# Where the blocks of w_down are staged in layer 1's feed-forward network

## The chip, the cores and the metric

The kernel runs on one core of one Trainium2 chip. The metric is the device time of one execution in microseconds (us), the median over several runs. The engines are TensorE (PE, with its weight loads shown apart as PEld), VectorE (DVE), ScalarE (ACT), GpSimd (POOL) and SyncE (SP, which here only issues DMAs).

## What is computed

Two layers of a diffusion transformer on 512 image tokens and 256 context tokens, model width 1024, in float32. Each layer is an attention and Fourier mixer followed by a feed-forward network (FFN) of width 2816. In layer 1, the last one, the context isn't updated, so that its FFN works on the 512 image tokens alone:

```python
def swiglu(h, w_gate, w_up, w_down):
    return (jax.nn.silu(h @ w_gate) * (h @ w_up)) @ w_down
...
x = x + gt2 * swiglu(rms_norm(x, g_ffn[l]) * (1 + sc2) + sh2, w_gate[l], w_up[l], w_down[l])
...
return rms_norm(x, g_final)
```

## The kernel before

Every float32 product is made of three products of float32r parts: each operand is split into a high part (ACT casts it, `split`, L103) and a low part (DVE subtracts, also L103), and `mm3` (L90) multiplies high by high, high by low and low by high.

`ffn` (L1638 on; it runs for layer 1 only, layer 0 has a function of its own) cuts the width 2816 into eleven blocks of 256. Of block p it needs 256 columns of w_gate, 256 columns of w_up and 256 rows of w_down, 1 MB each; they are called G(p), U(p) and D(p) here. The program's order for p = 1 to 10 is:

1. G(p) through `seven`: a Strassen product with seven products of 12 matmuls (256 columns moving), 84 in all, then Silu (L1680, L1682).
2. D(p-1) is loaded and split (`load_down`, `load_cols`), and `down(p-1)` multiplies it with `us`, the split activations of block p-1: eight products (d = 0 to 7) of 6 matmuls with 512 columns moving, each added to the residual tile `xt[d]` by DVE (L1663).
3. U(p) through `seven`, its results multiplied with the gate's, and split into the `us` of block p (L1695 and L103).

Block 0 is made by `first`, without `seven`; the last block's `down` is done in two halves with the final norm behind them. The order that the engines really follow is set by a scheduler when the program is built: it takes instructions by the program's order, but lets a later one go ahead on an engine when an earlier one isn't ready yet by its own model of time. The queues are then fixed. SP issues the loads in that fixed order too, and an issue waits until the tile that it writes is free.

Tiles around the change:

- `raw` (L116): [128, 2048] float32 (1 MB), a ring of two, `tag="raw", bufs=2`. In `ffn` every G, U and D block is loaded into it. `load_pair` takes one for G and U, and `load_cols` (L119) one for D. A `raw` is free again when its last part is split. For G and U that is late: `weights` (L1296) has POOL make sums of quarters in place in the `raw` (L1316 to L1318, L1324), and the seven parts are split one by one as the products come to them.
- `w` (L106): [128, 1024], a ring of ten. Each of the seven parts takes one tile; D takes four, from its split until the last product of its `down`.
- `s1` in `weights` is on tag `hf`, a ring of two. `utile` (tag `u`, a ring of eight) holds the activations.
- `xt[k]` (L1170, in `w_out`): eight residual tiles of [128, 768]. In layer 1 only columns 0 to 511 are loaded (L1173), changed or read. They lie in the pool `fp`, which takes the place of the attention's pool `at` when `w_out` begins; a tile of `fp` can be written when the tiles of `at` that lay at its address are done.

Of the kernel before, what the change touches and what calls it, by code (L numbers as in the profile page):

```python
# [9 lines left out]
F32 = mybir.dt.float32  # L10
# [7 lines left out]
P = 128  # L18
D = 1024
KB = D // P  # L20
SX = 512
SC = 256
T = SX + SC
# [23 lines left out]
class Builder:  # L47
# [68 lines left out]
    def raw(self):  # L116
        return self.wp.tile([P, 2048], F32, name=self.nm("raw"), tag="raw", bufs=2)

    def load_cols(self, src, nk, w, per, slots=None):  # L119

        hs = []
        krow = src.rearrange("(k p) w -> p k w", p=P)
        step = min(nk, (2048 // w) // per * per)
        for k0 in range(0, nk, step):
            kn = min(step, nk - k0)
            r = self.raw()
            rv = r[:, 0 : kn * w].rearrange("p (k w) -> p k w", w=w)
            self.queue(rv, krow[:, k0 : k0 + kn, :])
            for s in range(0, kn, per):
                h, l = (slots or self.whl)()  # L130
                n = min(per, kn - s)
                for j in range(n):
                    c = slice(j * w, (j + 1) * w)
                    self.split(h[:, c], l[:, c], r[:, (s + j) * w : (s + j + 1) * w])
                    hs.append((h[:, j * w : (j + 1) * w], l[:, j * w : (j + 1) * w]))
        return hs
# [1028 lines left out]
    def w_out(self, l, oh, ol):  # L1165

        nc = self.nc
        full = l < DEPTH - 1
        w = self.a["w_out"][l]
        xt = [self.fp.tile([P, T], F32, name=self.nm("xt"), tag=f"x{k}", bufs=1) for k in range(KB)]  # L1170
        e = T if full else SX
        for d in range(KB):
            nc.sync.dma_start(xt[d][:, 0:e], self.xsc[:, d, 0:e])  # L1173
        acc = self.fp.tile([P, T], F32, name=self.nm("acc"), tag="acc", bufs=1)
        hs = [self.utile(F32) for k in range(KB)]

        def one(d, wt, rng, s):
            r0, r1 = rng
            ps = self.mm()[:, 0 : r1 - r0]
            wh, wl = wt  # L1180
            self.mm3(ps, [(wh[:, k], wl[:, k], oh[k][:, r0:r1], ol[k][:, r0:r1]) for k in range(KB)])
            nc.vector.scalar_tensor_tensor(
                xt[d][:, r0:r1], ps, self.gt(l, 0, d, s), xt[d][:, r0:r1], op0=ALU.mult, op1=ALU.add
            )
            self.stat_add(acc, xt[d], rng, d)

        rngs = (XR,) if full else XH
        late = []
        for dp in range(KB // 2):
            rv = self.load_pair(w[:, dp * 256 : (dp + 1) * 256])  # L1190
            for j in range(2):
                d = 2 * dp + j
                wt = self.pair_half(rv, j)
                if d >= KB - LATE:
                    late.append((d, wt))
                    continue
                one(d, wt, XR, 0)
                if full:
                    one(d, wt, CR, 1)
        bcs = []  # L1200
        for rng, bank in zip(rngs, (self.fl, self.mm)):
            for d, wt in late:
                one(d, wt, rng, 0)
            bcs.append(self.stat_bc(acc, rng, bank()))
        hi, lo = self.act
        n = (T if full else SX) // 2
        last = []
        r0, r1 = rngs[0]
        for k in range(KB):
            shf = self.sh(l, 1, k, 0)  # L1210
            with self.tc.issue_after(last[-2]) if k > 1 else ExitStack():
                nc.vector.scalar_tensor_tensor(
                    hs[k][:, r0:r1], xt[k][:, r0:r1], self.sc(l, 1, k, 0), bcs[0], op0=ALU.mult, op1=ALU.mult
                )
            nc.scalar.activation(hi[k][:, 0:n], hs[k][:, 0:n], AF.Identity, bias=shf)
            last.append(
                nc.vector.scalar_tensor_tensor(
                    lo[k][:, 0:n], hs[k][:, 0:n], shf, hi[k][:, 0:n], op0=ALU.add, op1=ALU.subtract
                ).ins
            )  # L1220
        for k in range(KB):
            nc.scalar.activation(hs[k][:, r0:r1], hs[k][:, r0:r1], AF.Identity, bias=self.sh(l, 1, k, 0))
        if full:
            for d, wt in late:
                one(d, wt, CR, 1)
        for rng, bc in zip(rngs[1:], bcs[1:]):
            for k in range(KB):
                self.norm_raw(hs[k], xt[k], bc, rng, l, k, 0)
        if full:
            bc = self.stat_bc(acc, CR)  # L1230
            for k in range(KB):
                self.norm_raw(hs[k], xt[k], bc, CR, l, k, 1)
        return xt, hs
# [403 lines left out]
    def ffn(self, l, xt, hs):  # L1637
        nc = self.nc  # L1638
        full = l < DEPTH - 1
        wg, wu, wd = (self.a[n][l] for n in ("w_gate", "w_up", "w_down"))  # L1640
# [4 lines left out]
        cols = lambda p: slice(p * 256, (p + 1) * 256)  # L1645
# [23 lines left out]
                        nc.sync.dma_start(self.xsc[:, d, r0:r1], xt[d][:, r0:r1])  # L1669
            return done.ins  # L1670

        load_down = lambda p: self.load_cols(wd[cols(p), :], 2, D, 1)
        us = utiles()
        room = [[acc[:, j * n : (j + 1) * n]] * 2 for j in range(2)]
        parts = lambda j, cs, sl: self.split(us[j][0][:, cs], us[j][1][:, cs], sl)
# [2 lines left out]
        for p in range(1, npc):  # L1678
# [13 lines left out]
            if p < npc - 1:  # L1692
                for j in range(2):
                    e = slice(0 if j else n, 2 * n)
# [13 lines left out]
        p = npc - 1  # L1708
# [176 lines left out]
```

## Time and profile before

| | us |
|---|---|
| median of 3 runs | 1558.27 (1555.56 to 1558.91) |
| the profiled execution | 1555.41 |
| its span, first to last instruction | 1553.6 |
| layer 1's `w_out` and FFN, from 1139 us of the span to its end | 414.6 |
| of that, from block 1's U to the issue of block 10's D and a little behind | 1204 to 1503 |

The rows are read so: each names an engine, a line of the kernel, an operation and its tiles (what is written, an arrow, what is read), with its time. In square brackets stands the time that the engine stood idle before it, and what that idle time ended with. "PEclk" is the granted TensorE clock as a share of full speed. Matmuls overlap in the trace, so that a busy time of PE is not a measure of its load, but idle time of PE is idle.

### The profile page before, as it was taken

How to read it: one execution, taken by the hardware profiler on the slowest of the kernel's cores; microseconds unless marked ns; L12 is line 12 of the kernel's file. 1: busy time of each engine (PE TensorE's matmuls, PEld its weight loads, DVE VectorE, ACT ScalarE, POOL GpSimd, SP SyncE). 2: the span in 40 equal slices, each digit the busy share in tenths (PEclk: the TensorE clock that was granted, in tenths of full speed). 3: DMA queues.
4: the chain of work that ended last, by engine and by line, in shares of the span. 5: the costliest groups of instructions: out<-in, count | busy, mean ns of one | idle time of the engine just before them, and what ended most of it. 6: DMA issues, size and time to landing. Idle time of an engine off the chain costs nothing.

```text
span 1553.6 us, 25611 instructions
## 1 busy us (share of the span) xinstructions
PE 1485.4 (96%) x9769; PEld 1363.6 (88%) x9769; DVE 1133.1 (73%) x1907; ACT 763.9 (49%) x1542; POOL 556.7 (36%) x463
## 2 busy tenths in 40 slices
PE   6989989999999999999999998999999999999997
PEld 3789967688999999999899978987799898988987
DVE  3767577753978878876887866667749778777775
ACT  3556566642744444444435545666637344444344
POOL 0354345310256656452000025353401444344432
PEclk9999999999999999999999999999999999999999
DMA  9510085851133543446883541065441423223221
GB/s 339 197 48 29 1 263 159 290 190 29 54 130 130 163 138 123 161 137 227 307 301 110 167 128 35 28 201 189 141 134 52 136 82 109 83 82 126 92 82 55
DMA packets 124298, 211.59 MB, mean 136 GB/s; under 512 B 6456, under 2 KB 87120, under 8 KB 119056
## 3 DMA queue, kind: packets, MB, share of 16 engines
q1 hardware_dynamic: 116320, 203.92, 38.2%
q0 software_dynamic: 7856, 6.04, 2.0%
q8 instruction: 77, 1.26, 0.3%
q14 instruction: 45, 0.37, 0.1%
HBM read 180.96 MB, written 28.97 MB: 135 GB/s over the span
## 4 chain that ended last, share of the span: by engine, by line
PE 69%; DVE 10%; DMA 8%; ACT 4%; POOL 4%; issue 4%; SPq 1%; POOLq 0%; DVEq 0%; ACTq 0%
PE mm L90 15%; PE lg L90 14%; PE fl L90 13%; DVE w L103 5%; PE mm L1506 4%; PE mm L945 4%; PE lg L1506 4%; PE mm L937 2%; ACT w L103 2%; PE fl L278 2%; DMA raw<-in_w_up_dram 2%; PE lg L833 2%; PE lg L841 2%; DMA ra<-in_w_ada_dram 2%; PE fl L1506 1%
## 5 line engine op out<-in xcount | busy, mean ns | idle before, releaser
L103 DVE TENSOR_TENSOR w<-raw,w 128x512 fp32r<-128x512 f32 (+1 forms) x336 | 314.7, 949 | 113.5 <-ACT w L103 108.1
L103 ACT CAST w<-raw 128x512 fp32r<-128x512 f32 (+1 forms) x336 | 228.5, 701 | 316.4 <-POOL raw L1324 94.1
L90 PE MATMUL lg<-ahi,w 128*128 128x384 f32 (+1 forms) x640 | 151.2, 312 | 6.9 <-DVE w L103 3.1
L90 PE MATMUL fl<-ahi,w 128*128 128x384 f32 (+1 forms) x640 | 153.5, 308 | 0.9 <-ACT acc L1385 0.9
L852 POOL TENSOR_TENSOR p<-p,rc 128x768 f32<-128x768 f32 (+2 forms) x84 | 111.4, 1344 | 116.9 <-DVE rc L850 105.3
L90 PE MATMUL lg<-th,w 128*128 128x384 f32 (+1 forms) x640 | 150.4, 311 | 1.4 <-DVE u L1448 1.2
L90 PE MATMUL mm<-u,w 128*128 128x512 f32 (+1 forms) x576 | 137.9, 378 | 3.9 <-DVE u L103 2.2
L339 POOL TENSOR_TENSOR rs<-ms,mhalf 128x8 f32<-128x8 f32 (+3 forms) x22 | 28.6, 1304 | 288.7 <-DVE ms L335 288.7
L90 PEld LDWEIGHTS lg<-ahi,w 128*128 128x128 f32 x640 | 111.5, 191 | 11.2 <-ACT w L103 5.1
L90 PE MATMUL fl<-w,ahi 128*128 128x256 f32 x576 | 115.0, 293 | 5.9 <-DVE w L103 3.8
L90 PEld LDWEIGHTS mm<-u,w 128*128 128x128 f32 x576 | 98.0, 190 | 20.9 <-DVE u L103 3.5
L90 PEld LDWEIGHTS lg<-th,w 128*128 128x128 f32 x640 | 111.7, 191 | 3.3 <-DVE u L1448 1.5
L90 PEld LDWEIGHTS fl<-ahi,w 128*128 128x128 f32 x640 | 112.0, 190 | 2.5 <-ACT acc L1385 1.1
L90 PE MATMUL mm<-ahi,w 128*128 128x256 f32 (+1 forms) x448 | 107.1, 330 | 0.0
L1324 POOL TENSOR_TENSOR raw<-raw 128x512 f32<-128x512 f32 x40 | 62.3, 1559 | 110.8 <-DVE w L103 110.8
L90 PEld LDWEIGHTS fl<-w,ahi 128*128 128x128 f32 x576 | 93.5, 196 | 8.0 <-DVE w L103 4.3
L103 DVE TENSOR_TENSOR t<-mm,t 128x512 fp32r<-128x512 f32 x108 | 74.0, 687 | 34.7 <-ACT t L103 34.0
L90 PE MATMUL lg<-tl,w 128*128 128x384 f32 (+1 forms) x320 | 99.3, 310 | 0.0
L90 PE MATMUL lg<-alo,w 128*128 128x384 f32 (+1 forms) x320 | 99.2, 310 | 0.0
L1316 POOL TENSOR_TENSOR s<-raw 128x512 f32<-128x512 f32 x40 | 54.6, 1366 | 123.3 <-DMA raw<-in_w_up_dram 75.8
L90 PE MATMUL fl<-alo,w 128*128 128x384 f32 (+1 forms) x320 | 98.7, 308 | 0.0
L844 DVE TENSOR_REDUCE neg<-lg 128x1 f32<-128x768 f32 (+2 forms) x96 | 80.7, 851 | 19.9 <-PE lg L841 19.0
(367 smaller groups left out, 3980.7 us busy)
## 6 DMA issues: line engine op xcount, KB each, us to landing
raw<-in_w_ada_dram SPq DMA_DIRECT2D x40, 1024.0 KB, 4.9
raw<-in_w_gate_dram SPq DMA_DIRECT2D x22, 1024.0 KB, 5.2
raw<-in_w_up_dram SPq DMA_DIRECT2D x22, 1024.0 KB, 5.3
uh<-uh SPq DMA_DIRECT2D x33, 384.0 KB, 4.8
w<-uh SPq DMA_DIRECT2D x33, 384.0 KB, 4.6
wd<-in_w_down_dram SPq DMA_DIRECT2D x47, 256.0 KB, 5.1
raw<-in_w_in_dram SPq DMA_DIRECT2D x11, 1024.0 KB, 5.5
raw<-in_w_down_dram SPq DMA_DIRECT2D x11, 1024.0 KB, 4.8
```

The lines of the kernel that those rows point to most:

```text
L90: mm = lambda a, b, **k: self.nc.tensor.matmul(out, a, b, skip_group_check=more, **k)
L103: return self.nc.scalar.copy(hi, src).ins, self.nc.vector.tensor_sub(lo, src, hi).ins
L278: end = nc.tensor.matmul(st["ps"][o : o + 32, :], self.ct[:, k0 + i, :], rs[i][:, j], start=(k0 % hold == 0), stop=((k0 + by) % hold == 0) ...
L833: nc.tensor.matmul(o, qt[:, qs], K1[:, kv, k0 : k0 + w], start=True, stop=False)
L841: nc.tensor.matmul(o, qt[:, qs], K2[:, kv, k0 : k0 + w], start=False, stop=True)
L844: nc.vector.tensor_reduce(ng, lv, axis=AX.X, op=ALU.max, negate=True)
L852: nc.gpsimd.tensor_tensor(pt, pt, rc[:, i : i + 1].to_broadcast(list(pt.shape)), op=ALU.mult)
L937: nc.tensor.transpose(ps[:, col + j * P : col + (j + 1) * P], pt[:, c : c + P], self.ident)
L945: nc.tensor.matmul(out[:, r], V[:, kb, kv, :], t[:, c], start=first and n == 0, stop=end and n == len(todo) - 1,)
L1316: nc.gpsimd.tensor_add(s1, a21, a22)
L1324: nc.gpsimd.tensor_sub(a12, a12, a11)
L1506: nc.tensor.matmul(ps, w[:, x, c], u[:, y], start=(not more and k == 0 and j == 0), stop=(k == npc - 1 and j == 2), skip_group_check=True,)
```

## The change

D's blocks get a tile of their own, `rd`, [128, 2048], one buffer, on the pool `fp`; `load_cols` takes the function that makes the tile as an argument. G and U keep the ring of two between them. The eight residual tiles of layer 1 become 512 wide instead of 768, 1 KB less for each partition and tile, 8 KB in all, which is what `rd` takes (2048 float32).

```diff
-    def load_cols(self, src, nk, w, per, slots=None):
+    def load_cols(self, src, nk, w, per, slots=None, raw=None):
...
-            r = self.raw()
+            r = (raw or self.raw)()
...
-        xt = [self.fp.tile([P, T], F32, name=self.nm("xt"), tag=f"x{k}", bufs=1) for k in range(KB)]
         e = T if full else SX
+        xt = [self.fp.tile([P, e], F32, name=self.nm("xt"), tag=f"x{k}", bufs=1) for k in range(KB)]
...
-        load_down = lambda p: self.load_cols(wd[cols(p), :], 2, D, 1)
+        own = lambda: self.fp.tile([P, 2 * D], F32, name=self.nm("rd"), tag="rd", bufs=1)
+        load_down = lambda p: self.load_cols(wd[cols(p), :], 2, D, 1, raw=own)
```

## Rows read from the trace of the kernel before

**Rows 1.** The page: busy time of each engine, its share of the span, and its instructions.
```profile
PE 1485.4 (96%) x9769; PEld 1363.6 (88%) x9769; DVE 1133.1 (73%) x1907; ACT 763.9 (49%) x1542; POOL 556.7 (36%) x463
```
**Rows 2.** Busy time by stretch, from layer 1's w_out to the end, and four stretches of two blocks each, from one issue of a G to the next but one. Columns: the stretch, its length, then busy us (and instructions) of PE, PEld, DVE, ACT and POOL, the granted clock, the DMA engines' share, GB/s.
```profile
1139.00:1553.60 414.60, 394.75 (x2746) 366.14 (x2744) 314.27 (x502) 184.16 (x362) 146.25 (x114) 0.99 0.27 90
...
1206.72:1272.48 65.76, 62.90 (x416) 57.34 (x415) 48.40 (x73) 26.84 (x49) 25.62 (x20) 0.97 0.30 102
1272.48:1336.45 63.97, 63.12 (x434) 58.28 (x434) 51.24 (x75) 26.91 (x50) 27.32 (x20) 1.00 0.30 99
1336.45:1403.50 67.05, 64.62 (x434) 59.65 (x433) 51.01 (x75) 27.17 (x50) 27.12 (x20) 0.97 0.29 95
1403.50:1468.89 65.39, 63.44 (x434) 58.32 (x433) 51.70 (x75) 26.97 (x50) 27.78 (x20) 1.00 0.29 98
```
**Rows 3.** The order in time of SP's DMA issues, in the third of these stretches. The start of each, its length, the line, the tile and the source.
```profile
1333.01 0.37 SPq L142 DMA_DIRECT2D raw<-in_w_up_dram  x1
1336.45 0.37 SPq L142 DMA_DIRECT2D raw<-in_w_gate_dram  x1
1351.42 0.37 SPq L114 DMA_DIRECT2D raw<-in_w_down_dram  x1
1362.78 0.37 SPq L142 DMA_DIRECT2D raw<-in_w_up_dram  x1
1366.01 0.37 SPq L142 DMA_DIRECT2D raw<-in_w_gate_dram  x1
1382.42 0.37 SPq L114 DMA_DIRECT2D raw<-in_w_down_dram  x1
1400.06 0.37 SPq L142 DMA_DIRECT2D raw<-in_w_up_dram  x1
1403.50 0.37 SPq L142 DMA_DIRECT2D raw<-in_w_gate_dram  x1
```
**Rows 4.** DMA issues between 1204 and 1503 us: tile and source, KB of one, median us from issue to landing.
```profile
raw<-in_w_up_dram SPq DMA_DIRECT2D x10, 1024.0 KB, 5.0
raw<-in_w_down_dram SPq DMA_DIRECT2D x10, 1024.0 KB, 4.8
```
**Rows 5.** The order in time of what happens around the arrival of the U that was issued at 1362.78 us: the end of D's split before it, PE, POOL and ACT.
```profile
1364.77 1.22 DVE L103 TENSOR_TENSOR w<-raw,w 128x1024 fp32r<-128x1024 f32 x1
...
1367.18 1.42 PE L90 MATMUL mm<-u,w 128*128 128x512 f32 x5 [0.72 <-DVE u L103]
...
1368.94 1.28 POOL L1316 TENSOR_TENSOR s<-raw 128x512 f32<-128x512 f32 x1 [2.36 <-DMA raw<-in_w_up_dram]
1368.97 0.62 ACT L103 CAST w<-raw 128x512 fp32r<-128x512 f32 x1 [3.79 <-DMA raw<-in_w_up_dram]
...
1369.64 0.39 PE L90 MATMUL lg<-ahi,w 128*128 128x256 f32 x1 [1.03 <-ACT w L103]
```
**Rows 6.** Busy time by stretch at five arrivals of a U and behind two of them; columns as in rows 2.
```profile
1234.00:1239.00 5.00, 2.63 (x14) 1.57 (x12) 4.04 (x5) 1.48 (x3) 1.44 (x2) 1.00 0.73 228
1239.00:1242.00 3.00, 2.82 (x15) 2.26 (x16) 2.84 (x2) 1.17 (x4) 2.84 (x3) 0.87 0.92 317
1242.00:1245.00 3.00, 3.00 (x17) 3.00 (x17) 0.16 (x1) 1.37 (x3) 2.92 (x3) 0.56 0.01 3
...
1303.00:1306.00 3.00, 2.16 (x13) 1.46 (x11) 2.62 (x3) 1.69 (x4) 2.67 (x2) 1.00 0.95 322
...
1366.00:1371.00 5.00, 2.57 (x11) 1.49 (x11) 3.53 (x5) 1.68 (x4) 2.56 (x3) 0.99 0.89 301
1371.00:1374.00 3.00, 3.00 (x13) 2.81 (x14) 1.45 (x1) 0.39 (x1) 2.92 (x3) 0.50 0.01 2
...
1434.00:1438.00 4.00, 2.41 (x10) 1.42 (x10) 3.46 (x5) 1.68 (x4) 2.50 (x3) 1.00 1.04 336
...
1498.00:1503.00 5.00, 3.41 (x19) 2.33 (x18) 4.57 (x6) 1.69 (x4) 3.60 (x3) 1.00 0.95 327
```
**Rows 7.** PE alone by stretch, two stretches that lie between such arrivals: length, busy us, granted clock, the DMA engines' share, GB/s.
```profile
1272.50:1301.40 28.90, 28.90 (x201) 1.00 0.32 107
1336.50:1366.00 29.50, 29.50 (x207) 1.00 0.32 104
```
**Rows 8.** Who waited for whom between 1160 and 1553 us: the engine and line that waited, for what, us in total, times, the longest.
```profile
POOL s L1316 <- DMA raw<-in_w_up_dram: 47.4, 10, 9.2
...
ACT w L103 <- POOL raw L1324: 36.8, 18, 3.8
ACT w L103 <- DMA raw<-in_w_up_dram: 30.8, 10, 3.8
ACT w L103 <- PE lg L90: 23.5, 17, 2.9
```
**Rows 9.** The order in time at the next D, the one that was issued at 1382.42 us: the first cast and the last subtraction of its split.
```profile
1399.03 1.04 ACT L103 CAST w<-raw 128x1024 fp32r<-128x1024 f32 x1
...
1402.26 1.21 DVE L103 TENSOR_TENSOR w<-raw,w 128x1024 fp32r<-128x1024 f32 x1
```
**Rows 10.** The order in time where layer 1's residual tiles are loaded and first used.
```profile
1125.04 10.69 SPq L1173 DMA_DIRECT2D xt<-xsc  x8
...
1137.55 0.75 DVE L1182 SCALAR_TENSOR_TENSOR xt<-mm,ada,xt 128x512 f32<-128x512 f32 x1 [5.69 <-PE mm L90]
```
**Rows 11.** The order in time on PE where the last block's `down` begins.
```profile
1529.50 3.97 PE L90 MATMUL mm<-u,w 128*128 128x256 f32 x27 [0.48 <-ACT u L103]
```

## The prediction

> **What bounds the kernel now.** I read the page first: PE is busy for 96% of the span and DVE for 73% [rows 1]. PE is the bound, so that only PE's idle time and lost clock can be won. Next the busy time by stretch: layer 1's last part takes 414.6 us, of which PE is idle for 19.9, and four stretches of two blocks each take 65.76, 63.97, 67.05 and 65.39 us, with PE idle for 2.86, 0.85, 2.43 and 1.95 us and a granted clock of 0.97 in two of them [rows 2]. The reader is to see that the stretches differ though their work is the same.
>
> Third, SP's issues in time [rows 3]. The ring of two `raw` is handed on without a pause. The U at 1333.01 keeps its `raw` until D takes it at 1351.42 (18.4 us); the G at 1336.45 keeps its own until the next U at 1362.78 (26.3); that D until the next G at 1366.01 (14.6). Then 19.6, 34.1 and 21.1 us for the next three. These six stays add up to 134.1 us, and on two buffers that is 67.05 us, the whole stretch. So nothing is loaded ahead: each U is asked for only when G's last part, or in the other parity D's, has left a buffer.
>
> Fourth, what that costs PE. The U issued at 1362.78 lands some 5.0 us later [rows 4]. POOL, ACT and, behind the cast, PE wait for it: PE starts on U at 1369.64 after 1.03 us of idleness, and had already stood for 0.72 us at 1367.18, where only `down` was left to it and DVE was still splitting `us` [rows 5]. By stretch, the five places of this kind have PE idle for 2.37 + 0.18 (1234 to 1242), 0.84 (1303), 2.43 (1366), 1.59 (1434) and 1.59 us (1498): 9.0 in all. Behind two of them PE runs at a lower granted clock: 3 us at 0.56 and 3 us at 0.87 after 1239, 3 us at 0.50, the lower of the clock's two levels (1.2 GHz), after 1371, that is 1.32 + 0.39 + 1.50 = 3.2 us lost [rows 6]. Between such places PE has no idle time: 28.90 of 28.90 us and 29.50 of 29.50, at full clock [rows 7]. Over layer 1's FFN, POOL waited for a U ten times, 47.4 us in total, and ACT ten times, 30.8 us [rows 8]; those are engines that aren't the bound, and only the 9.0 us are PE's.
>
> **The change part by part.** *D leaves the ring.* The number of loads, splits, sums and matmuls stays what it is; only when loads may start changes. Without D's stays, 134.1 - 14.6 - 21.1 = 98.4 us are left on two buffers, 49.2 us for two blocks. That is below what PE needs for them, so the ring stops being the bound even if every stay is some 25% longer. In the trace, U could have been issued when the earlier U left, at 1351.42 in place of 1362.78, and so landed at about 1356.5, some 10 us before PE runs out of other work at 1366; the next G at 1362.78 in place of 1366.01.
>
> How much is that? What PE needs for two blocks I take from the stretch with the least idleness: 63.12 us busy, at clock 1.00 [rows 2]. Four stretches: 4 x 63.12 = 252.5 us against 262.17 (1206.72 to 1468.89), a gain of 9.7. The fifth place, at 1498, lies behind them and gives 1.6. Sum: 11.3 us. Adding up the places instead gives 9.0 + 3.2 = 12.2, the most there is. I take 11.3, since the first way leaves some small waits standing.
>
> *D in its single tile.* A D may be loaded only when the one before has been split. That split ends at 1364.77 + 1.22 = 1365.99 [rows 5], the next D would land by 1371 (4.8 us [rows 4]), and its own first cast comes only at 1399.03 [rows 9]. Some 28 us hide it, and its cost is nothing; with that cover gone it would be up to 4.8 us for each block. Behind D's issue in SP's queue stand the next U and G, whose buffers come free at 1382 and 1400 [rows 3], so an issue that waits until 1366 holds nobody up.
>
> The Trainium skill ("Trainium Kernel Development and Optimization", Best Practices) says to double-buffer, so that DMA overlaps compute; it speaks against a single tile, and by it the loads would be exposed. The rows just read don't bear it out here, since the other work between two D lies between load and use; it is rival 4.
>
> *The ring of w.* ACT already waits for PE to give up a tile there, 17 times, 23.5 us [rows 8]. D's four tiles of ten are held from its split to the end of its `down`. An earlier D can be split earlier and hold them longer. The trace shows no such case. From below: nothing, as G and U keep six of ten; from above: PE misses one part of each `seven` by the 0.84 us that it waited at 1303 [rows 6], 20 times, 16.8 us. I take zero, because in the stretches without waits [rows 7] four tiles are held by D as well, and PE still doesn't stand.
>
> *Narrower residual tiles.* No instruction changes, since only 512 columns were ever moved. What lies behind `xt` moves to other addresses, and so waits for other tiles of the attention. The first issue is at 1125.04, and DVE first uses `xt` at 1137.55 after it waited 5.69 us for PE, not for the load [rows 10]. The last of the eight issues comes by 1135.73; if the first had to wait that long it would land at 1140.8, 3.3 us late. Below, nothing is to be won, because nobody waited. I take zero and keep the 3.3 us for the range.
>
> *The tail.* The last `down` starts with 0.48 us of idleness while ACT splits the last `us` [rows 11]; none of that hangs on a load, so it moves forward as a whole.
>
> What is late next? PE itself, and behind it DVE: 51 us in 63 [rows 2].
>
> **The rivals.** 1. *The split of `us` takes the place of the load.* PE's 0.72 us at 1367.18 was a wait for DVE's split, not for U. If the fixed order puts `down` ahead of U at every block, ten waits of about 0.75 us stay: 7.5 of the 11.3, and the gain is 3.8: 1554.5 us. For it: the program names `down` before U. Against it: where U was there in time, no such wait is left [rows 7].
>
> 2. *The change doesn't do what it says.* If the scheduler puts the next D ahead of U in SP's queue, that issue waits for D's split, until 1366, and U is as late as before, or later: 1558 us. For it: program order. Against: the scheduler has let G and U go by their readiness already, as U stands right before the next G in the queue [rows 3].
>
> 3. *The ring of w, the slower side.* Place: the splits in `seven`. Price: the 16.8 us above, less the gain: 1558.3 + 5.5 = 1563.8. It decides from the point where one D is split while the four tiles of the D before are still held, so that G and U have two tiles for a product of 12 matmuls. For it: ACT's 23.5 us of waits for PE. Against: the splits of G and U come before the next D's in the program, and are ready more often once their loads are early.
>
> 4. *The single tile exposes D.* Ten times 4.8 us, less the gain: 1558.3 + 48 - 11.3 = 1595. It decides from the point where a D is split less than 5 us before the next is needed; the rows show 28 us [rows 9].
>
> **How the numbers follow.** The profiled execution took 1555.41 us, 2.9 less than the median of 1558.27 and near the fastest of the three. By its own time the forecast is 1555.4 - 11.3 = 1544.1; by the median, which is what is compared, 1558.3 - 11.3 = 1547.0. If the 2.9 us come from more clock lost at the same places, they go as well. Chances: the forecast 0.60, rival 1 0.15, rival 2 0.11, rival 3 0.11, rival 4 0.03. Faster by more than 0.2% (3.1 us, about what a measurement of this kernel can tell from no change) are the forecast and rival 1: 0.75; within it rival 2: 0.11; slower rivals 3 and 4: 0.14. The range: at its lower end all 12.2 us from the median and the 2.9 us largely too, against small new waits: 1542. At its upper end the forecast with 3.3 us for the residual tiles (1550.3), rival 1 and rival 2: 1558.5. Rivals 3 and 4 are left out.
>
> **What would show it.** In the changed kernel's trace: SP issues each U some 10 us or more before PE's first product of it; POOL's and ACT's waits for a U shrink from 47.4 and 30.8 us to a few; the stretches of two blocks come down to 63 to 64 us with the granted clock at 1.00; PE's idleness in the four of them falls from 8.1 to about 1 us, and the part before `w_out` is unchanged. Wrong would be: waits of PE for DVE's `us` at each block (rival 1), U's still issued right behind a D (rival 2), or more and longer waits of PE for the splits of `w` (rival 3).

## The result

The median fell from 1557.01 us (1555.56 to 1558.91, 4 runs) to 1548.52 us (1547.32 to 1550.48, 4 runs): a ratio of 0.9946 [0.9928, 0.9964], 8.5 us less by the medians. Forecast were 1547.0 us and a gain of 11.3. The profiled execution of the changed kernel took 1550.48 us, with a span of 1548.7. It is the slowest of its four, and everything ahead of layer 1's `w_out` ran later in it than in the profile of before, though the two kernels do the same there: the first load of `xt` is issued at 1127.54 us against 1125.04 [rows 10]. I therefore measure from that issue to the last addition into `xt`: 419.40 us before and 411.97 after, 7.43 less.

The busy times of the page hardly differ from [rows 1], as it should be: the same work is done, in less time.

```profile
PE 1485.8 (96%) x9769; PEld 1362.4 (88%) x9769; DVE 1121.1 (72%) x1907; ACT 763.5 (49%) x1542; POOL 553.6 (36%) x463
```

SP's issues of the changed kernel, in order of time, over one stretch of two blocks; the counterpart of [rows 3]:

```profile
1331.02 0.37 SPq L142 DMA_DIRECT2D raw<-in_w_gate_dram  x1
1334.45 0.37 SPq L114 DMA_DIRECT2D rd<-in_w_down_dram  x1
1347.99 0.37 SPq L142 DMA_DIRECT2D raw<-in_w_up_dram  x1
1363.13 0.37 SPq L142 DMA_DIRECT2D raw<-in_w_gate_dram  x1
1367.17 0.37 SPq L114 DMA_DIRECT2D rd<-in_w_down_dram  x1
1379.06 0.37 SPq L142 DMA_DIRECT2D raw<-in_w_up_dram  x1
```

Now U is asked for when the earlier U leaves its `raw` (1347.99), some 15 us before PE runs out of other work; before, it was 1362.78 [rows 3]. D's issue follows each G by 3.4 to 4.0 us.

Who waits for a load, in the changed kernel, from 1160 to 1553 us; the columns are those of [rows 8]:

```profile
POOL s L1316 <- DMA raw<-in_w_gate_dram: 36.3, 8, 7.3
...
ACT w L103 <- PE lg L90: 31.6, 20, 4.5
ACT w L103 <- PE mm L90: 26.7, 11, 5.7
POOL s L1316 <- DMA raw<-in_w_up_dram: 23.4, 8, 4.9
```

POOL's waits for a U are half of what they were, and ACT's 30.8 us for a U [rows 8] are no longer in the list. POOL now waits for each G as well, so that its waits for loads grew in sum, from 49.1 us (47.4 and 1.7) to 59.7; that holds up nothing by itself, as the next list shows. ACT's waits for PE to give up a `w` grew.

What PE itself waited for, from 1130 to 1548 us (us in total, times, the longest):

```profile
PE mm L90 <- DVE u L103: 2.8, 3, 0.9
PE lg L90 <- DVE w L103: 1.9, 4, 0.6
PE mm L1380 <- ACT ahi L103: 1.6, 1, 1.6
```

No load stands there. The waits for DVE are rival 1's in a smaller dose, and the last line was not thought of. Where they lie is seen by stretch. I divide the loop at the same event in both kernels, the last addition of `down(1)`, `down(3)`, `down(5)`, `down(7)` and `down(9)` into `xt`, since the issues of G moved against the work. Columns as in [rows 2]; before:

```profile
1265.24:1328.67 63.43, 62.58 (x430) 57.74 (x429) 50.70 (x75) 26.92 (x50) 27.72 (x21) 1.00 0.30 100
1328.67:1395.70 67.03, 64.60 (x434) 59.63 (x433) 50.98 (x75) 27.17 (x50) 27.11 (x21) 0.97 0.29 95
1395.70:1461.10 65.40, 63.45 (x434) 58.33 (x433) 51.71 (x76) 26.97 (x50) 27.78 (x21) 1.00 0.30 97
1461.10:1525.58 64.48, 62.89 (x433) 58.03 (x432) 50.03 (x74) 26.58 (x48) 22.63 (x17) 1.00 0.25 83
```

and after:

```profile
1262.50:1326.72 64.22, 63.59 (x437) 58.44 (x436) 49.42 (x75) 27.14 (x50) 25.97 (x21) 1.00 0.31 99
1326.72:1391.60 64.88, 63.52 (x434) 58.21 (x433) 49.34 (x76) 26.95 (x50) 26.14 (x21) 1.00 0.30 98
1391.60:1456.30 64.70, 63.36 (x434) 58.16 (x433) 49.59 (x75) 26.94 (x50) 26.12 (x21) 1.00 0.30 98
1456.30:1520.20 63.90, 62.57 (x429) 57.61 (x428) 47.86 (x73) 26.56 (x48) 18.68 (x15) 1.00 0.20 67
```

The clock is whole and the stretches are now alike, but each still has 0.6 to 1.4 us of idle time in it. Eight blocks take 257.70 us instead of 260.34, only 2.64 less. Most of the gain lies earlier: `down(1)` ends 134.96 us behind the first `xt` issue instead of 140.20. The stretches don't hold quite the same work, since the orders on PE differ: the changed kernel has seven matmul records more in the first (437 against 430) and four fewer in the last (429 against 433). The matmuls here mostly follow each other at 0.12 us, so that this is up to some 0.8 us at the start and 0.5 at the end, an estimate.

One of the places that are left, around 1364 us, in order of time. PE goes over from one block's products to the next there; I call that a handover, and it is at every second one that PE stands:

```profile
1363.32 1.22 DVE L103 TENSOR_TENSOR w<-rd,w 128x1024 fp32r<-128x1024 f32 x1
1363.48 1.65 POOL L1355 TENSOR_TENSOR u<-u 128x256 f32<-128x256 f32 x1 [2.39 <-DVE u L1354]
1364.42 0.39 PE L90 MATMUL mm<-u,w 128*128 128x512 f32 x1
1364.45 1.22 DVE L103 TENSOR_TENSOR u<-u,u 128x512 fp32r<-128x512 f32 x1
1365.73 0.73 PE L90 MATMUL mm<-u,w 128*128 128x512 f32 x2 [0.92 <-DVE u L103]
1365.93 1.21 DVE L103 TENSOR_TENSOR w<-rd,w 128x1024 fp32r<-128x1024 f32 x1
1367.07 0.68 DVE L103 TENSOR_TENSOR w<-raw,w 128x512 fp32r<-128x512 f32 x1
1367.80 0.50 PE L90 MATMUL lg<-ahi,w 128*128 128x256 f32 x2 [0.41 <-DVE w L103]
```

It is the place of [rows 5]. The load has landed (the U issued at 1347.99 is first multiplied at 1366.30), and what comes late is DVE: D's split, the split of `us` behind it, D's second half, and only then the first part of the next block. PE stands 0.92 us for `us` and 0.41 for `w`.

The wait for `ahi` lies ahead of the loop, in the norm of the second half of the columns. PE by stretch (length, busy, clock, DMA share, GB/s), and the order in time there, after:

```profile
1186.00:1188.00 2.00, 0.40 (x3) 1.00 0.00 0
1188.00:1191.00 3.00, 2.93 (x16) 0.68 0.00 0
1191.00:1194.00 3.00, 3.00 (x22) 0.75 0.02 5
```

```profile
1178.19 1.11 DVE L1217 SCALAR_TENSOR_TENSOR alo<-u,ada,ahi 128x256 fp32r<-128x256 f32 x1
...
1178.98 1.48 POOL L1316 TENSOR_TENSOR s<-raw 128x512 f32<-128x512 f32 x1
...
1182.14 1.28 POOL L1317 TENSOR_TENSOR raw<-raw 128x512 f32<-128x512 f32 x1
1182.28 1.70 DVE L103 TENSOR_TENSOR w<-raw,w 128x512 fp32r<-128x512 f32 x1
...
1187.82 0.50 PE L1380 MATMUL mm<-ahi,w 128*128 128x256 f32 x2 [1.60 <-ACT ahi L103]
```

The same split on DVE, PE's pause and PE's stretch behind it, before:

```profile
1179.20 0.69 DVE L103 TENSOR_TENSOR w<-raw,w 128x512 fp32r<-128x512 f32 x1
1184.79 0.39 PE L1381 MATMUL mm<-alo,w 128*128 128x256 f32 x1 [0.56 <-DVE alo L103]
1185.50:1188.50 3.00, 3.00 (x28) 1.00 0.03 5
```

U(1) is issued at 1172.98 us instead of 1204.16, so POOL makes its sums (L1316, L1317) in the middle of the norm. DVE's operations beside them take 1.11 and 1.70 us (0.47 and 0.69 before, where no sum of POOL runs beside them), the normed half comes late, and PE stands for 1.60 us where before it had 0.56. Its granted clock is lower in the six us behind, 3 x 0.32 + 3 x 0.25 = 1.7 us more; before, it was 1.00 there.

### The profile page after: what moved, and what is told of

Read it like the earlier page. It is cut to its first block, busy times and chain, and to the rows that moved or that the text cites. A ratio compares the mean times of both kernels' runs of the same rounds, so it can differ in the third digit from the quotient of the medians.

```text
span 1548.7 us, 25590 instructions
## 1 busy us (share of the span) xinstructions
PE 1485.8 (96%) x9769; PEld 1362.4 (88%) x9769; DVE 1121.1 (72%) x1907; ACT 763.5 (49%) x1542; POOL 553.6 (36%) x463
## 3 DMA queue, kind: packets, MB, share of 16 engines
q8 instruction: 77, 1.26, 0.3%
## 4 chain that ended last, share of the span: by engine, by line
PE 70%; DVE 12%; issue 5%; POOL 5%; ACT 4%; DMA 4%; SPq 0%; POOLq 0%; DVEq 0%; ACTq 0%
PE mm L90 15%; PE fl L90 12%; PE lg L90 12%; DVE w L103 5%; PE mm L1506 4%; PE mm L945 4%; PE lg L1506 4%; PE fl L278 3%; PE mm L937 2%; ACT w L103 2%; PE lg L833 2%; PE lg L841 2%; PE fl L1506 1%; POOL raw L1324 1%; PE lg L522 1%
## 5 line engine op out<-in xcount | busy, mean ns | idle before, releaser
L103 DVE TENSOR_TENSOR w<-raw,w 128x512 fp32r<-128x512 f32 (+1 forms) x314 | 279.7, 904 | 105.7 <-ACT w L103 100.8
L103 ACT CAST w<-raw 128x512 fp32r<-128x512 f32 (+1 forms) x314 | 206.6, 677 | 291.9 <-POOL raw L1324 102.7
L1316 POOL TENSOR_TENSOR s<-raw 128x512 f32<-128x512 f32 x40 | 54.2, 1354 | 143.1 <-DMA raw<-in_w_gate_dram 58.7
```

The lines of the kernel that those rows point to most:

```text
L103: return self.nc.scalar.copy(hi, src).ins, self.nc.vector.tensor_sub(lo, src, hi).ins
L1316: nc.gpsimd.tensor_add(s1, a21, a22)
```

## The experiments

The theory behind the forecast: D's stays in the ring made each U late, and a single tile for D is enough. Its rivals are that the narrower `xt` did it, that the single tile costs something, and that D in particular, and not one claimant too many (a claimant is a kind of load that takes its buffer from the ring), was the trouble. A second question came with the result: where the rest of the 11.3 us went, 3.9 by the profiles and 2.8 by the medians. In the table all times count from the first `xt` issue: the end of `down(1)`, the eight blocks from there to the end of `down(9)`, and the last addition into `xt`. The ratio is to runs of the kernel before that were made beside the variant's.

| | `down(1)` | eight blocks | last | ratio |
|---|---|---|---|---|
| before | 140.20 | 260.34 | 419.40 | 1 |
| changed kernel | 134.96 | 257.70 | 411.97 | 0.9946 [0.9928, 0.9964] |
| e1, `xt` alone | 140.33 | 259.25 | 418.43 | 1.0002 [0.999, 1.0014] |
| e6, D in two tiles | 134.82 | 257.97 | 412.09 | 0.9955 [0.9937, 0.9973] |
| e7, U in its own tile | 135.34 | 259.18 | 413.81 | 0.995 [0.9934, 0.9966] |
| e2, U(1) held | 136.72 | 249.48 | 405.50 | 0.9909 [0.9894, 0.9924] |
| e3, D's splits outside the ring of w | 138.86 | 254.33 | 413.48 | 0.9965 [0.9952, 0.9979] |
| e4, e2 and e3 | 136.56 | 253.99 | 410.84 | 0.9953 [0.9939, 0.9967] |
| e8, first parts outside the ring of w | 136.08 | 259.87 | 415.26 | 0.9981 [0.9972, 0.999] |
| e10, D's low part on POOL | 135.84 | 274.46 | 433.29 | 1.0086 [1.007, 1.0101] |
| e11, D's split behind `us` | 135.14 | 257.62 | 412.07 | 0.9959 [0.9943, 0.9975] |
| e12, U(2) held | 136.16 | 258.27 | 413.73 | 0.9964 [0.9952, 0.9977] |
| e13, e2 and e11 | 136.55 | 257.39 | 413.25 | 0.9975 [0.9964, 0.9985] |
| e15, line 1355 on DVE | 140.02 | 251.32 | 413.82 | 0.9951 [0.9937, 0.9965] |

**e1_xt_only: the kernel before with the narrower residual tiles alone.**

```diff
-        xt = [self.fp.tile([P, T], F32, name=self.nm("xt"), tag=f"x{k}", bufs=1) for k in range(KB)]
         e = T if full else SX
+        xt = [self.fp.tile([P, e], F32, name=self.nm("xt"), tag=f"x{k}", bufs=1) for k in range(KB)]
```

> The kernel before with only the residual tiles of layer 1 cut to 512 columns; D still shares the ring of two with G and U. It tells whether the narrower tiles alone do anything. My theory (the gain is D's leaving the ring): the same as before within 0.2%, with PE idle at the arrivals of U as before (about 9 us in all), because no engine's order of instructions differs. Rival (other addresses, and so other waits for the attention's tiles, carry part of the gain): 2 us or more faster or slower.

Measured: 1557.15 us against 1556.22, ratio 1.0002. The narrower tiles alone do nothing; the gain comes with D's own tile.

**e6_rd2: two tiles for D.**

```diff
-        own = lambda: self.fp.tile([P, 2 * D], F32, name=self.nm("rd"), tag="rd", bufs=1)
+        own = lambda: self.fp.tile([P, 2 * D], F32, name=self.nm("rd"), tag="rd", bufs=2)
```

The room for it comes from tiles of `utile` and of the token splits, made for 512 tokens in layer 1 instead of 768, which were never used beyond that.

> The changed kernel with two tiles for the blocks of w_down in place of one; the room comes from split tiles of u, and their neighbours, being 512 columns wide, which changes no instruction. Theory (a single tile is enough, since a block lies loaded for some 28 us between its split and its first use): the same as the changed kernel, ratio 0.992 to 0.997 to the kernel before, PE's waits unchanged, each D issued one block earlier. Rival (a load that can't overlap the use of the block before is exposed, so double-buffering gains): faster than the changed kernel by some us in the loop of seven blocks, under 222 us from down(2) to down(9) against 226.6.

Measured: ratio 0.9955, the eight blocks in 257.97 us against 257.70, and PE's waits the same. The second tile buys nothing; rival 4 is refuted in both of its forms, as a loss and as a gain left lying.

**e7_u_own: U in the tile of its own, D back in the ring with G.**

```diff
-        load_down = lambda p: self.load_cols(wd[cols(p), :], 2, D, 1, raw=own)
+        load_down = lambda p: self.load_cols(wd[cols(p), :], 2, D, 1)
...
-                wu[:, cols(p)], toks, n, *m, lambda o, ps: nc.vector.tensor_tensor(o, ps, g[0][:, 0:n], op=ALU.mult)
+                wu[:, cols(p)], toks, n, *m, lambda o, ps: nc.vector.tensor_tensor(o, ps, g[0][:, 0:n], op=ALU.mult), own
```

> The changed kernel with the roles turned: the blocks of w_up have the tile of their own, those of w_down go back to the ring of two with w_gate. PE's instructions come in the same order as in the changed kernel. Theory (the ring had one claimant too many, whichever it is): as fast as the changed kernel, ratio 0.992 to 0.997, seven blocks in 225 to 228 us. Rival (D in particular had to leave, since it is held until DVE has split it): at least 5 us slower than the changed kernel, ratio about 1.00.

Measured: ratio 0.995, within 2 us of the changed kernel at each point. So it wasn't D's stay as such: three claimants shared two buffers, and it is enough that either of these two leaves.

**e2_hold_u1: the work on U(1) in `seven` (its sums and products) held, in the fixed order, behind POOL's last sum for G(1).** It was to take the new wait ahead of the loop away.

```diff
-                    nc.gpsimd.tensor_sub(a12, a12, a11)
+                    self.third = nc.gpsimd.tensor_sub(a12, a12, a11).ins
...
+            with self.after(*([self.third] if p == 1 else [])):
                 self.seven(
```

> The changed kernel, with POOL's sums for U(1) held behind POOL's last difference for G(1) in POOL's order. It tests the new stall before the loop: PE 1.6 us idle at 1186 us and 1.7 us of lost clock behind it. My theory: U(1), which now lands early, sends POOL to work beside DVE, DVE's instructions take 1.1 and 1.7 us in place of 0.5 and 0.7 us, and the norm of the second half comes late by over a microsecond. So with the sums held back the idle time at this place returns to about 0.6 us at full clock, and the kernel gains 1.5 to 2.7 us on the changed one (0.991 to 0.994 of before). Rival (the place is a matter of the fixed order on PE, which changed there too, or of the run): no gain, idle time 1 us or more stays.

Measured: 1543.97 us (1542.52 to 1545.62), ratio 0.9909, faster than both kernels; but not for the reason that I gave. The wait near 1188 us is indeed down to 0.56 us, yet another of 3.05 us opened behind it (DVE and PE in order of time):

```profile
1203.28 1.76 DVE L103 TENSOR_TENSOR w<-raw,w 128x512 fp32r<-128x512 f32 x1
1204.96 3.25 DVE L103 TENSOR_TENSOR tl<-u,th 128x256 fp32r<-128x256 f32 x3
...
1209.26 0.48 PE L90 MATMUL lg<-ahi,w 128*128 128x256 f32 x1 [3.05 <-DVE u L1347]
```

and `down(1)` ends 1.8 us later than in the changed kernel. The gain is in the eight blocks, where the columns are those of [rows 2]:

```profile
1265.88:1328.21 62.33, 62.33 (x434) 58.13 (x433) 49.41 (x75) 27.30 (x50) 25.69 (x21) 1.00 0.33 102
1328.21:1390.55 62.34, 62.34 (x434) 58.15 (x433) 49.52 (x76) 27.38 (x50) 25.37 (x21) 1.00 0.32 102
1390.55:1452.88 62.33, 62.33 (x434) 58.14 (x433) 50.34 (x75) 27.38 (x50) 25.22 (x21) 1.00 0.32 102
```

PE has no idle time at all in these three stretches, so 62.33 us is enough for two blocks. The constraint on one block had changed the fixed order of the later ones: in the place that answers to 1364 us, PE has other products left until 1366.4, and the split of `us` takes 0.68 us and is done at 1365.2. It begins ahead of POOL's sum of line 1355 (1364.66 us), which in the changed kernel it stood behind; the delay falls on D's second half instead (1.76 us from 1365.10), and PE isn't waiting for that yet. DVE in order of time:

```profile
1363.02 1.23 DVE L103 TENSOR_TENSOR w<-rd,w 128x1024 fp32r<-128x1024 f32 x1 [0.18 <-ACT w L103]
1364.17 0.41 DVE L1354 TENSOR_TENSOR u<-u,lg 128x256 f32<-128x256 f32 x1
1364.50 0.68 DVE L103 TENSOR_TENSOR u<-u,u 128x512 fp32r<-128x512 f32 x1
```

**e3_own_w and e4_both: D's four split tiles outside the ring of w; and that together with e2.** The token tiles and `utile` are made for 512 tokens there, for room.

```diff
-        load_down = lambda p: self.load_cols(wd[cols(p), :], 2, D, 1, raw=own)
+        part = lambda: self.fp.tile([P, D], F32R, name=self.nm("wd"), tag="wd", bufs=4)
+        load_down = lambda p: self.load_cols(wd[cols(p), :], 2, D, 1, slots=lambda: (part(), part()), raw=own)
```

> The changed kernel, with the four split tiles of D in tiles of their own, so that the ring of ten holds parts of G and U alone; the room comes from narrower activation and token tiles in layer 1. It tests what is left at the handover from one block to the next, 1.3 us of PE's idle time in each second block. My theory (rival 3 in a small dose: G's and U's parts can't be split ahead because D's split takes four of ten tiles and stands before them in DVE's queue): PE's idle time in the loop falls from 4.4 to 1.5 us or less, and the kernel gains some 3 us on the changed one (0.991 to 0.994 of before). Rival (rival 1: down stands before U in PE's order and waits for the split of the activations, whatever the ring): 0.9 us of idleness for DVE's split of the activations stays at each second block, and the time is that of the changed kernel.

> e2 and e3 together. If both terms are what I think and add up: 4 to 6 us less than the changed kernel (0.990 to 0.991 of before, some 1543 us). If only one of the two theories holds, the time of that one alone.

Measured for e3: eight blocks in 254.33 us, 3.4 less than the changed kernel, but `down(1)` 3.9 later, since in the fixed order that came out PE waits longer for `us` there (1130 to 1552 us; the 2.8 us stand at 1246.06):

```profile
PE mm L90 <- ACT u L103: 3.2, 2, 2.8
```

Ratio 0.9965. With both edits 0.9953: 3.7 us less in the eight blocks, 1.6 more ahead of them and 1.0 more behind them (20.29 us against 19.31). So what comes with D's leaving the ring of `w` in the loop is lost again before and after it, in e3 wholly and in e4 for the greater part, and the loop isn't as good as in e2.

**e8_first_own: the first split part of each G and U outside the ring of w.**

```diff
+        one = lambda: self.fp.tile([P, 1024], F32R, name=self.nm("w1"), tag="w1", bufs=2)
...
-            w = self.slot(F32R).rearrange("p (i k w) -> p i k w", i=2, k=4)
+            w = (self.slot(F32R) if out or self.e > SX else one()).rearrange("p (i k w) -> p i k w", i=2, k=4)
```

> The changed kernel with the first of the three split tiles of each G and U taken from two tiles of their own and not from the ring of ten w. Theory (what is left at each second handover is that U's first part is split late, because its tile comes free late and DVE's split of it stands behind those of D): PE finds U's first part ready, the loop of seven blocks falls from 226.6 to 219 to 222 us, ratio 0.990 to 0.993. Rival (the wait is for DVE's split of us behind D's in DVE's queue, and stays): loop 225 to 228 us, ratio 0.993 to 0.997.

Measured: eight blocks in 259.87 us, 2.2 more than the changed kernel, ratio 0.9981. The first part is ready now, and PE waits for `us` instead, and longer: 6.0 us in four waits between 1240 and 1490 us. The theory isn't borne out: a free `w` isn't what was lacking, as far as a kernel with another fixed order can tell. DVE's splits are slower (0.983 us for a part of 128x512 over that stretch; 0.819 in the changed kernel).

**e10_d_pool: D's low part subtracted on POOL.**

```diff
-    def split(self, hi, lo, src):
-        return self.nc.scalar.copy(hi, src).ins, self.nc.vector.tensor_sub(lo, src, hi).ins
+    def split(self, hi, lo, src, eng=None):
+        return self.nc.scalar.copy(hi, src).ins, (eng or self.nc.vector).tensor_sub(lo, src, hi).ins
...
-                    self.split(h[:, c], l[:, c], r[:, (s + j) * w : (s + j + 1) * w])
+                    self.split(h[:, c], l[:, c], r[:, (s + j) * w : (s + j + 1) * w], self.nc.gpsimd if raw else None)
```

> The changed kernel with the low part of each D's split computed on POOL and not on DVE, so that two operations of 1.22 us for each block leave DVE's queue just where the split of us stands behind them. Theory (what is left at each second handover is DVE's queue): PE's wait for us goes, the loop of seven blocks falls from 226.6 to 220 to 223 us, ratio 0.990 to 0.993. Rival (POOL slows DVE while both work, and its longer operation delays the sums of G and U): no gain or a loss, loop 226 to 232 us, ratio 0.995 to 1.00.

Measured: 1570.22 us, ratio 1.0086, the eight blocks in 274.46 us. The operation, 1.22 us on DVE, takes 2.67 on POOL, where half that size (line 1316, 128x512) takes 1.29 at best in the changed kernel, so that POOL's own pace is most of it (groups by line, 1240 to 1490 us: busy us, mean ns, idle time before and its end):

```profile
L103 POOL TENSOR_TENSOR w<-rd,w 128x1024 fp32r<-128x1024 f32 x14 | 37.3, 2671 | 10.3 <-ACT w L103 10.3
```

and PE's waits for DVE's `us` grew to 11.2 us in nine (1130 to 1570 us; 2.8 in three in the changed kernel), so DVE wasn't relieved by it.

**e11_us_first: D's split held behind the split of the first half of `us`.**

```diff
+                    cut = self.split(v(us[j][0]), v(us[j][1]), swap(m[j]) if j else both(m[j]))
+                    self.cut = cut[1] if j == 0 else self.cut
...
+            with self.after(*([self.cut] if p > 1 else [])):
+                wd2 = load_down(p - 1)
```

> The changed kernel with the splits of each D held, in the fixed order, behind the split of the first half of the us that its down uses. Theory (what is left at each second handover, some 1.3 us of PE's idle time, comes from DVE's queue, in which a D's split of 1.22 us stands ahead of the split of us): PE's wait for DVE's us at 1364 us goes, two blocks fall from 64.8 to 63 us or less, ratio 0.990 to 0.993. Rival (the split of us is late because its own inputs are late, and the order on DVE changes nothing): two blocks stay at 64 to 65 us, ratio 0.994 to 0.997. Third: D's split then comes late itself and PE waits for that instead, ratio above 0.996.

Measured: the wait for `us` is gone, as the theory said, and the time is not: eight blocks in 257.62 us, ratio 0.9959. D's two splits now stand ahead of line 1360, and PE waits for that (1240 to 1490 us):

```profile
PE mm L90 <- DVE u L1360: 2.9, 3, 1.0
PE lg L90 <- DVE u L1347: 1.7, 4, 0.6
```

So it is not this one order on DVE. A burst of work falls to DVE at each second handover, and in both orders PE waits for what stands last in it.

**e12_hold_u2 and e13_hold_us: e2's constraint on block 2; and e2 with e11.**

```diff
-            with self.after(*([self.third] if p == 1 else [])):
+            with self.after(*([self.third] if p == 2 else [])):
```

> As the kernel that holds U(1)'s products behind POOL's last sum for G(1), but with the constraint on block 2 instead of block 1. The entry into the loop is then that of the changed kernel (PE idle 1.6 us near 1188). Theory (the gain of holding U(1) came from the fixed order that the scheduler then finds for the later blocks, not from the entry): the order of the later blocks changes here too, and two blocks in the loop take either 62.3 us as there (ratio 0.988 to 0.992) or 64.8 as in the changed kernel (0.994 to 0.997), as the order falls out. Rival (it came from the entry alone): ratio 0.994 to 0.997 whatever the order.

> Both constraints together: U(1) held behind POOL's last sum for G(1), and the splits of each D behind that of the first half of us. If the two act on different waits, PE has no idle time in the loop already from the first, and the second adds nothing: two blocks at 62.3 us, ratio 0.990 to 0.992. If the second delays D's split, PE waits for D: ratio above 0.993.

Measured: 0.9964 and 0.9975, eight blocks in 258.27 and 257.39 us. Neither comes near e2's 249.48. Of e13's two outcomes it is the second: PE waits 4.5 us, in five waits, for line 1360 behind D's splits. It has the held U(1) of e2, its entry too (`down(1)` at 136.55 against 136.72), and not its loop; so e2's loop comes from the order found for the later blocks, and a held U(1) alone doesn't bring it. e12 is what its theory and its rival both allow, and tells nothing apart: the later order didn't change in it as the theory had thought, and PE's waits for DVE's `us` are those of the changed kernel, 2.8 us in three.

**e15_c22_dve: the sum of line 1355 on DVE instead of POOL.**

```diff
-        (nc.vector if n > 256 else nc.gpsimd).tensor_add(c22, c22, c21)
+        nc.vector.tensor_add(c22, c22, c21)
```

> The changed kernel with the sum of line 1355 (128x256, one for each Strassen product) on DVE and not on POOL. Theory (at the second handover DVE's split of us takes 1.22 us and not 0.68 because POOL's sum runs at that moment): the split takes 0.68 us, POOL's 1.65 us between DVE's lines 1354 and 1360 become one of 0.41 on DVE, PE's wait falls from 1.34 us for two blocks to 0.5 or less: two blocks in 62.3 to 63.9 us, ratio 0.989 to 0.993. Rival (DVE's work in that burst is what PE waits for, and 0.41 us more of it, or another fixed order, gives the same wait elsewhere): two blocks in 64.2 to 65 us, ratio 0.994 to 0.998.

Measured: eight blocks in 251.32 us, 6.4 less than the changed kernel, though some 2.4 of that is work that here comes only after `down(9)`; the first six blocks, in the rows below, take 189.61 us against 193.80. PE alone by stretch (length, busy, clock, DMA share, GB/s):

```profile
1266.64:1329.28 62.64, 62.03 (x427) 1.00 0.31 101
1329.28:1392.73 63.45, 63.07 (x436) 1.00 0.30 100
1392.73:1456.25 63.52, 62.85 (x434) 1.00 0.32 100
```

and the split of `us` takes 0.69 us in the place of 1.22 (at 1398.39 us). In the loop that bears the theory out, though the fixed order differs too and has its part. The ratio is 0.9951 all the same: the new order loses 5.1 us ahead of `down(1)`, where PE waits up to 1.9 us for ACT's split of a `w`, and 3.2 in the last `down` (22.48 us from `down(9)` to the end against 19.31, with 2.43 us more of busy time in it).

## Why the prediction was right, and where it wasn't

**What bounds the kernel.** Right. With one claimant less on the ring, loads come early and PE waits for none. e1 leaves `xt` out as a cause, e7 shows that it need not be D that leaves. The place at 1234 to 1242 us [rows 6] is gone: PE is busy for 10.87 of the 11 us from 1234 to 1245, and the clock behind is at 1.00.

The sum of the stays that was read for it shows less than it seems to. A stay was counted from one issue into a buffer to the next into the same buffer; counted so, the stays on two buffers always add up to twice the stretch. They do in the changed kernel too: U's of 33.79 and 31.07 us and G's of 32.11 and 32.75 make 129.72 (U's issues at 1314.20, 1347.99 and 1379.06, G's at 1331.02, 1363.13 and 1395.88), half of which is 64.86, the whole stretch, and each load is still issued within 0.1 us of the split that frees its buffer. So the stays of G and U did not remain at 98.4 us, as the 49.2 us had it; they grew by 32%, beyond the 25% that were allowed for. What changed is how far a load lies ahead of its use: a U is first multiplied 18 us behind its issue (1347.99 to 1366.30), before it was 7 (1362.78 to 1369.64 [rows 5]). That sign came as forecast. POOL's waits for a U, which were to shrink to a few us, are at 23.4.

**The sum.** By the same events as above, the places of [rows 6] against what was saved:

| stretch | places of [rows 6] in it | upper sum | saved |
|---|---|---|---|
| first `xt` issue to `down(0)` | none | 0 | -1.07 |
| to `down(3)` | 1234 to 1245, 1303 | 4.26 + 0.84 = 5.10 | 5.52 |
| to `down(9)` | 1366 to 1374, 1434, 1498 | 3.93 + 1.59 + 1.59 = 7.11 | 3.43 |
| to the end | none | 0 | -0.45 |
| sum | | 12.2 | 7.43 |

The forecast took 11.3 of the 12.2, and called 12.2 the most there is; the second row has more than its places, so that they weren't all. The row to the end holds a little more work: 156 matmul records, before it was 152. The step that failed is "what is late next? PE itself". It was DVE at each second handover: 1.33 to 1.36 us of idle time stay in each of the last three stretches (64.88 - 63.52, 64.70 - 63.36, 63.90 - 62.57), where I had left some tenths. This is rival 1's mechanism, not at every block as rival 1 had it but at every second, with 0.92 us for `us` and 0.41 for the part of `w` behind it. I had seen 0.72 us of it in [rows 5] and counted it among the 9.0 that the load would give back; it belonged to DVE.

**The floor.** I took 63.12 us for two blocks, the busy time of the best stretch [rows 2]. e2 needs 62.33 with the same 434 matmul records as that stretch. I read the 0.8 us between as waits that count as busy: the matmul ahead of the pause at 1364.42 is drawn 0.39 us long, and where three follow each other (0.85 us at 1366.53) each of the later two adds only 0.23, so that a pause hides some 0.16 us. That this makes up all of the 0.8 was only argued. The two errors had opposite signs: the gain that was there to be had is larger than I said (260.34 - 249.48 = 10.9 us in eight blocks), and the change took a smaller part of it. That the forecast time lies only 1.5 us from the measured one, while the gain is off by 2.8, is luck: with one run more, the median of before came out 1.26 us lower than the one from which the forecast was counted.

**D's single tile.** Right: e6 is the same within its interval. The Trainium skill's advice to double-buffer ("Trainium Kernel Development and Optimization", Best Practices) would have had e6 faster; it measured 0.9955 against 0.9946.

**The ring of w.** Costed at nothing, between 0 and 16.8 us. ACT waits for PE to give up a tile 58.3 us now (31.6 + 26.7; before it was 44.2, the 23.5 of [rows 8] and 20.7 for `mm`), but PE waits for the split of a `w` only 1.9 us in all, and e8, which has the first of these parts outside the ring, gains nothing. Rival 3 did not come about. e3 has 3.4 us less in eight blocks without D in the ring, under another fixed order.

**Narrower residual tiles.** Right: DVE first uses `xt` 12.5 us behind the first issue in both, [rows 10] and 1140.08 - 1127.54 in the changed kernel.

**The entry.** Not in the forecast at all. I asked what is queued behind SP's earlier issues, but not what POOL does with a block that is issued 31 us earlier (1172.98 against 1204.16): it makes its sums at once, beside DVE's norm. PE lost 1.6 us and 1.7 us of clock there, against 0.56 before, and 1.07 us of it are left at the end of `down(0)`. In e2 the same sums came later and hit the next thing, for 3.05 us.

**What stays open.** Which feature of e2's order frees PE at the second handover. e11 shows that it isn't D's split ahead of `us` alone; e15 that POOL's sum has a part in it; both change the rest of the order too, and a kernel with the changed kernel's order and only POOL's sum taken away wasn't tried.

Two rivals of the main reading stand as well. The change altered the fixed order on every engine, and not only the time of the loads: SP has D(0) ahead of block 0's G (1137.86 us), where before it stood behind G(1) (1170.45). e2 shows that an order alone can be worth 8 us in eight blocks, so it isn't shown how much of the 7.43 us is owed to early loads and how much to the new order; no kernel has the order of before with D outside the ring. And `rd` is one buffer more as well as one claimant less: a ring of three buffers for G, U and D, in the same room, wasn't tried.

## What to carry to other kernels

Where each load of a shared ring is issued the moment that a buffer comes free, and the engine that bounds the kernel stands when the load lands, a buffer for one of the claimants can pay, and here either of two would do. Judge it by how far each load lies ahead of its first use; the stays from issue to issue add up to the whole loop in any such ring, also in one that holds nobody up. Then ask what the earlier load sets going: the engine that prepares it starts at once, and takes its place in front of, or beside, work that was on the critical path. An idle time that ended with the load may still hide a second wait right behind; count as gain only what lies beyond that one, and take PE's floor from a kernel without pauses, not from the best stretch of one that has them.

## What the runs showed of the hardware

DVE's operations with two operands in SBUF become slower while POOL works, those that read PSUM don't. Groups by line of the changed kernel, 1262 to 1520 us (busy us, mean ns, idle time):

```profile
L103 DVE TENSOR_TENSOR w<-raw,w 128x512 fp32r<-128x512 f32 x93 | 73.7, 802 | 32.5 <-ACT w L103 32.2
L1663 DVE SCALAR_TENSOR_TENSOR xt<-mm,ada,xt 128x512 f32<-128x512 f32 x65 | 47.9, 743 | 10.2 <-PE mm L90 10.1
...
L1347 DVE TENSOR_TENSOR u<-u,lg 128x256 f32<-128x256 f32 x16 | 6.6, 411 | 0.7 <-PE lg L90 0.6
```

Line 1347 (one operand in PSUM) takes 0.41 us always and line 1663 0.74, while the splits, 0.68 us where POOL stands, come to a mean of 0.802 and to 1.70 at worst in the rows above. Sorted by what POOL does at the time, from 1140 us to the end: 94 splits of 128x512 with no instruction of POOL beside them take 0.67 to 0.69 us, 64 with one 1.04 in the mean and up to 1.82; line 1663's 38 with POOL beside them stay at 0.73 to 0.75. Around 1364 us one can see how: D's split runs from 1363.32 to 1364.54; POOL's sum, begun at 1363.48, ends at 1365.13, 0.59 us behind that; the split of `us`, begun at 1364.45, ends at 1365.67, 0.54 us behind POOL. Each finishes nearly as if it had begun when the other ended, 0.14 us sooner (without the other they take 0.73 and 0.68 us). The Trainium skill says so ("SBUF — State Buffer", Who interferes with whom): the ports that DVE and GpSimd share are an exclusive lock, a DVE instruction with two SBUF inputs contends for it with a GpSimd instruction that reads SBUF, and the order of issue decides who is blocked. These rows agree with it. It is why a POOL that starts early is not free although POOL is busy for 36% of the span. In e10, which lost 14 us against before, it may have its part beside POOL's slower pace; the two weren't told apart.
